# One attention layer on one core: q and k of a head pair in one PSUM bank, scores over 64 partitions, another start of the program

## The chip, the cores and the metric

The kernel runs on 1 core of a Trainium2 chip. The metric is device time in microseconds (us). The kernel before has 152.06 us as the median of 3 runs (151.92 to 152.91). Its profiled execution took 152.84 us, of which the span of the trace, from the first to the last instruction, is 151.1 us.

## The reference

One layer on a sequence of 256 rows, width 1024, 16 heads of 64:

```
hn   = rms_norm(x, norm_g)                 # x: (256, 1024) float32
q, k, v, z = split(hn @ w_in, 4)           # w_in: (1024, 4096)
s    = q k^T / 8 - slope_h * (t - s)       # causal, per head
o    = softmax(s) v
y    = x + (o * silu(z)) @ w_out           # w_out: (1024, 1024)
out  = rms_norm(y, final_g)
```

The sequence is one block of 256, so the choice of blocks in the reference never comes into play: every query sees its own block alone.

## The kernel before

Products are taken in float32 accuracy: each float32 operand is split into a high part, rounded to the type fp32r (ACT copies it), and a low part, the rest (DVE subtracts). A product is then three matmuls: high times high, high times low, low times high.

The work goes in four stages. **v**: x is transposed on PE (line 311), scaled by the norm weights `gT` on ACT (line 330) and split; eight rows of the v weights, 512 KB each, are loaded, split (lines 255 and 258) and multiplied, twelve products of 512 columns a row (lines 266 to 268). **z**: eight units of 128 columns of the gate weights, each 24 products of 256 columns (lines 271 to 273). **q, k and attention**: eight pairs of heads. A pair has a unit of q and a unit of k, 24 products each; then scores, softmax on DVE and ACT, transposes of the probabilities (line 447), the product with v (line 454). **o**: eight rows of `w_out`, their products cut into pieces of 512 and 256 columns, then the residual, the last norm and the stores.

How scores are made before: ACT rounds q, scaled by -1/8, into the tile `qq` on its own 64 partitions (line 399), DVE puts the low part of q on the other 64 partitions of the same tile (line 404). ACT rounds k into `kk` (line 408), a DMA on SP's queue copies `kk` to the other 64 partitions (line 412), DVE makes the low part `kl` (line 415), whose other half holds zeros. One matmul over 128 partitions then gives high and low part of q times the high part of k (line 424) and a second one high q times low k (line 425). Each head has two blocks (128 by 128, and 128 by 256), so a pair has 8 matmuls. q and k of a pair lie in two of three banks.

The order on every engine is written by a planner (`Plan`, lines 30 to 103): each piece of work has an engine, an estimated cost, a due time and what it reads and writes; the planner plays this through and the program is recorded in that order. Each engine then runs its own list strictly in order. SP's list holds most of the DMA issues, so an issue that waits holds those behind it.

Before the first product PE runs nine matmuls on a tile of zeros (`warm`, line 301), then transposes the norm weights (line 305) and the first quarter of x (line 311). The loads at the start are, on SP, the first quarter of x for rows 0 to 127 and the first weights; on ACT, the norm weights `gr` and then the first quarter of x for rows 128 to 255.

Of the kernel before, what the change touches and what calls it, by code (L numbers as in the profile page):

```python
# [22 lines left out]
EPS = 1e-6  # L23
MASKED = 3.0e38
HALF = (slice(0, DH), slice(DH, P))
# [81 lines left out]
def hybrid_trunk(ctx: ExitStack, tc: tile.TileContext, x, norm_g, w_in, w_out, final_g, out):  # L107
# [17 lines left out]
    def sb(name, shape, dtype=F32):  # L125
        return one.tile(shape, dtype, name=name)
# [18 lines left out]
    wl = [sb(f"wl{i}", [P, D], F32R) for i in range(NSPL)]  # L145
    NQ = 2
    qq = [sb(f"qq{i}", [P, 2, S], F32R) for i in range(NQ)]
    sb("pad3", [P, 16])
    kk = [sb(f"kk{i}", [P, 2, S], F32R) for i in range(NQ)]
    kl = [sb(f"kl{i}", [P, 2, S], F32R) for i in range(NQ)]  # L150
    NN = 3
# [7 lines left out]

    nc.sync.dma_start(xs[0][:, :256], x2[0:P, :256])  # L160
    nc.scalar.dma_start(gr, norm_g[0].rearrange("(t p) -> t p", p=P))
    nc.scalar.dma_start(xs[1][:, :256], x2[P:, :256])
    for i in range(2):
# [20 lines left out]
    def make_bias(h):  # L184
        nc.scalar.activation(bias[:, h, :], dist, AF.Copy, scale=2.0 ** (-8.0 * (h + 1) / H))

# [96 lines left out]

    def cols_unit(key, u, b, due):
        s = spl[key, u]
        h_, l_ = (w[s].rearrange("p (t e) -> p t e", t=ND) for w in (wh, wl))

        def step(g):
            for d in (2 * g, 2 * g + 1):
                mm3_cols(bank[b][:, :S], h_[:, d, :], l_[:, d, :], nh[:, d, :], nlo[:, d, :], d == 0, d == ND - 1)  # L290
        for g in range(4):
            add(T, 0.683, due + 0.683 * g, lambda g=g: step(g), split_of(s) + [("n", g)], [("b", b)], lat=0.25)
# [6 lines left out]
    slot["v", 0] = next_raw()  # L299
    for i in range(9):  # L300
        add(T, 0.21, -2000 + i, lambda: nc.tensor.matmul(bank[7][:, :256], warm[:, :P], warm, start=True, stop=True),
            [], [("b", 7)])

# [19 lines left out]

    add(T, 0.1, FIRST + 1, g_transpose, ["gr"], [("b", 6)], lat=0.25)
    add(V, 0.17, 0, lambda: nc.vector.tensor_copy(gT, bank[6][:, :ND]), [("b", 6)], ["gT"])
    for c in range(4):
        add(T, 0.45, FIRST if c == 0 else V0 + 2 * ROW * c - 2.3, lambda c=c: x_transpose(c), [("x", c, 0), ("x", c, 1)], [("b", 4 + c % 2)], lat=0.25)
        for d in (2 * c, 2 * c + 1):
# [49 lines left out]
    for i in range(ND):  # L378
        start = Z0 + UNIT * i
        if i % 2 == 0:  # L380
            load_cols("z", i, 3 * D + i * P, start - 12)
        split("z", i, cols_of("z", i), start, grid=ND)
        b = 4 + i % 2
        cols_unit("z", i, b, start)
        add(A, 0.42, start + UNIT + 1, lambda i=i, b=b: nc.scalar.activation(zs[:, i, :], bank[b][:, :S], AF.Silu),  # L385
            [("b", b), "silu"], [("zs", i)])
        if i == 0:
            add(G, 1.0, 5.0, make_dist, [("gh", 1)], ["dist"])
            for k in range(NQ):
                add(G, 0.5, 6.0 + k, lambda k=k: nc.gpsimd.memset(kl[k].bitcast(F32), 0.0), [("gh", 1)], [("kl", k), ("kl", k, 0), ("kl", k, 1)])  # L390
        for h in (2 * i, 2 * i + 1):
            add(A, 0.4, Z0 + 1.3 * h, lambda h=h: make_bias(h), ["dist"], [("bias", h)])
# [8 lines left out]
    def lo_q(p, b):  # L401
        t = qq[p % NQ]
        for a in range(2):
            nc.vector.scalar_tensor_tensor(t[HALF[1 - a], a, :], bank[b][HALF[a], :S], -(DH ** -0.5),
                                           t[HALF[a], a, :].bitcast(F32), op0=OP.mult, op1=OP.subtract)

    def hi_k(p, b, a):
        nc.scalar.copy(kk[p % NQ][HALF[a], a, :], bank[b][HALF[a], :S])  # L408
# [5 lines left out]
    def lo_k(p, b, a):  # L414
        nc.vector.tensor_sub(kl[p % NQ][HALF[a], a, :], bank[b][HALF[a], :S],  # L415
                             kk[p % NQ][HALF[a], a, :].bitcast(F32))

    def scores(p):

        for a in range(2):  # L420
            for o, q, k in ((slice(0, 128), slice(0, 128), slice(0, 128)),
                            (slice(128, 384), slice(128, 256), slice(0, 256))):
                l = qq[p % NQ][:, a, q]
                nc.tensor.matmul(bank[4 + a][:, o], l, kk[p % NQ][:, a, k], start=True, stop=False)  # L424
                nc.tensor.matmul(bank[4 + a][:, o], l, kl[p % NQ][:, a, k], start=False, stop=True)  # L425

    def softmax_max(p, a):
        for i, (o, b) in enumerate(BLK):
            nc.vector.tensor_tensor_reduce(nl[p % NN][:, a, o], bank[4 + a][:, o], bias[:, 2 * p + a, b], scale=1.0,  # L429
                                           scalar=3.0e38, op0=OP.add, op1=OP.min,  # L430
                                           accum_out=st[p % NN][:, 0, a, i:i + 1])
# [25 lines left out]
    for p in range(NP):  # L457
        base = A0 + PAIR * p
        if p % 2 == 0:
            load_cols("q", p, p * P, base - 12)  # L460
            load_cols("k", p, D + p * P, base - 9)
        bq, bk = (2 * p) % 3, (2 * p + 1) % 3
        split("q", p, cols_of("q", p), base, grid=ND)
        split("k", p, cols_of("k", p), base + UNIT, grid=ND)
        cols_unit("q", p, bq, base)
        cols_unit("k", p, bk, base + UNIT)
        E = base + 2 * UNIT + 0.3
        L = E - (0, 0, 0, 0, 0, 0, 3, 9)[p]
        n, m = p % NQ, p % NN
        add(A, 0.81, base + UNIT + 0.9, lambda p=p, b=bq: hi_q(p, b), [("b", bq)], [("qh", n)])  # L470
        add(V, 0.84, base + UNIT + 1.9, lambda p=p, b=bq: lo_q(p, b), [("b", bq), ("qh", n)], [("ql", n)])
        for a in range(2):
            add(A, 0.38, L + 0.4 + 0.4 * a, lambda p=p, b=bk, a=a: hi_k(p, b, a), [("b", bk)], [("kh", n, a)])
            add(Q, 0.2, L + 0.8 + 0.4 * a, lambda p=p, a=a: dup_k(p, a), [("kh", n, a)], [("kd", n, a)])
            add(V, 0.42, L + 1.0 + 0.4 * a, lambda p=p, b=bk, a=a: lo_k(p, b, a), [("b", bk), ("kh", n, a)],
                [("kl", n, a)])
        add(T, 0.97, FIRST + E, lambda p=p: scores(p),
            [("qh", n), ("ql", n)] + [(w, n, a) for w in ("kh", "kd", "kl") for a in range(2)] + [("kl", n)],
            [("b", 4), ("b", 5)], lat=0.25, slack=0.3)
        for a in range(2):  # L480
# [131 lines left out]
```

## Time and profile before

| | us |
|---|---|
| median of 3 runs | 152.06 |
| the profiled execution | 152.84 |
| its span | 151.1 |
| PE busy | 139.9 (93%) |
| DVE busy | 100.8 (67%) |
| ACT busy | 98.0 (65%) |
| POOL busy | 12.5 (8%) |

PE is TensorE's matmuls, PEld its weight loads. A matmul is pipelined: its own duration holds the way through the array, so what a matmul costs in a stream is the distance from its start to the start of the next one. In a timeline a row gives start, duration, engine, line, operation, tiles and shape, and in brackets how long the engine stood idle before it and what ended that.

### The profile page before, as it was taken

How to read it: one execution, taken by the hardware profiler on the slowest of the kernel's cores; microseconds unless marked ns; L12 is line 12 of the kernel's file. 1: busy time of each engine (PE TensorE's matmuls, PEld its weight loads, DVE VectorE, ACT ScalarE, POOL GpSimd, SP SyncE). 2: the span in 40 equal slices, each digit the busy share in tenths (PEclk: the TensorE clock that was granted, in tenths of full speed). 3: DMA queues.
4: the chain of work that ended last, by engine and by line, in shares of the span. 5: the costliest groups of instructions: out<-in, count | busy, mean ns of one | idle time of the engine just before them, and what ended most of it. 6: DMA issues, size and time to landing. Idle time of an engine off the chain costs nothing.

```text
span 151.1 us, 2711 instructions
## 1 busy us (share of the span) xinstructions
PE 139.9 (93%) x996; PEld 126.2 (84%) x996; DVE 100.8 (67%) x214; ACT 98.0 (65%) x217; POOL 12.5 (8%) x21
## 2 busy tenths in 40 slices
PE   7299999999999999999979999999999999999930
PEld 4178888889999999999959988998999788788820
DVE  0194899898534415686898786996867991653580
ACT  3294979888733617685974986779688863911240
POOL 6000010000000000000003001103010020150110
PEclk9999999999999999999999999999999999999995
DMA  4999999979886446717912481171000100000033
GB/s 115 336 401 404 369 369 348 348 248 284 258 255 157 149 105 209 245 35 196 386 47 93 184 274 43 35 278 34 9 20 17 39 0 0 0 0 4 0 139 139
DMA packets 18109, 24.82 MB, mean 164 GB/s; under 512 B 936, under 2 KB 15536, under 8 KB 18096
## 3 DMA queue, kind: packets, MB, share of 16 engines
q1 hardware_dynamic: 17792, 24.25, 49.3%
q10 hardware_dynamic: 304, 0.40, 0.8%
q8 instruction: 8, 0.13, 0.4%
q14 instruction: 5, 0.04, 0.1%
HBM read 22.55 MB, written 1.05 MB: 156 GB/s over the span
## 4 chain that ended last, share of the span: by engine, by line
PE 82%; DMA 7%; issue 3%; ACT 2%; DVE 1%; POOLq 0%; ACTq 0%; POOL 0%; DVEq 0%
PE bank L271 14%; PE bank L273 14%; PE bank L272 13%; PE bank L266 9%; PE bank L267 9%; PE bank L268 9%; DMA kk<-kk 5%; PE bank L454 4%; PE bank L447 3%; DMA xs<-in_x_dram 3%; PE bank L424 3%; PE bank L425 2%; PE bank L311 1%; ACT xs L542 1%; POOLq L607 0%
## 5 line engine op out<-in xcount | busy, mean ns | idle before, releaser
L258 DVE TENSOR_TENSOR wl<-raw,wh 128x1024 fp32r<-128x1024 f32 (+1 forms) x41 | 48.5, 1196 | 21.4 <-ACT wh L255 21.2
L271 PE MATMUL bank<-nh,wh 128*128 128x256 f32 x192 | 54.7, 285 | 0.0
L273 PE MATMUL bank<-nh,wl 128*128 128x256 f32 x192 | 53.5, 279 | 0.0
L272 PE MATMUL bank<-nlo,wh 128*128 128x256 f32 x192 | 53.5, 279 | 0.0
L255 ACT CAST wh<-raw 128x1024 fp32r<-128x1024 f32 (+1 forms) x41 | 41.5, 1026 | 0.9 <-PE bank L267 0.8
L271 PEld LDWEIGHTS bank<-nh,wh 128*128 128x128 f32 x192 | 36.0, 188 | 0.8 <-issue 0.7
L272 PEld LDWEIGHTS bank<-nlo,wh 128*128 128x128 f32 x192 | 36.0, 188 | 0.1
L273 PEld LDWEIGHTS bank<-nh,wl 128*128 128x128 f32 x192 | 36.1, 188 | 0.0
L266 PE MATMUL bank<-wh,gh 128*128 128x512 f32 (+1 forms) x72 | 28.2, 391 | 1.1 <-ACT wh L255 1.1
L267 PE MATMUL bank<-wh,gl 128*128 128x512 f32 (+1 forms) x72 | 27.2, 377 | 0.0
L268 PE MATMUL bank<-wl,gh 128*128 128x512 f32 (+1 forms) x72 | 27.1, 376 | 0.0
L266 PEld LDWEIGHTS bank<-wh,gh 128*128 128x128 f32 x72 | 14.1, 196 | 3.8 <-ACT wh L255 1.5
L499 POOL TENSOR_TENSOR gl<-gt,gh 128x256 fp32r<-128x256 f32 x8 | 8.3, 1032 | 106.2 <-ACT gh L497 106.2
L435 ACT ACTIVATE nl<-nl,st 128x128 f32<-128x128 f32 (+1 forms) x32 | 14.2, 447 | 3.2 <-DVE st L429 3.2
L268 PEld LDWEIGHTS bank<-wl,gh 128*128 128x128 f32 x72 | 13.9, 193 | 2.8 <-DVE wl L258 0.3
L267 PEld LDWEIGHTS bank<-wh,gl 128*128 128x128 f32 x72 | 14.0, 194 | 2.0
L385 ACT ACTIVATE zs<-bank 128x256 f32<-128x256 f32 x8 | 3.1, 385 | 11.5 <-PE bank L273 11.5
L429 DVE CUSTOM_DVE_ANT_0 nl<-bank,bias 128x128 f32<-128x128 f32 (+1 forms) x32 | 9.6, 352 | 0.7 <-PE bank L425 0.5
L491 ACT COPY pT<-bank 128x384 f32<-128x384 f32 x16 | 7.0, 483 | 4.0 <-PE bank L447 3.8
L408 ACT CAST kk<-bank 64x256 fp32r<-64x256 f32 x16 | 5.9, 367 | 5.2 <-PE bank L273 4.6
L415 DVE TENSOR_TENSOR kl<-bank,kk 64x256 fp32r<-64x256 f32 x16 | 6.8, 422 | 3.2 <-ACT kk L408 2.4
L399 ACT ACTIVATE qq<-bank 64x256 fp32r<-64x256 f32 x16 | 6.0, 377 | 4.1 <-PE bank L273 3.8
(66 smaller groups left out, 139.5 us busy)
## 6 DMA issues: line engine op xcount, KB each, us to landing
raw<-in_w_in_dram SPq DMA_DIRECT2D x12, 1024.0 KB, 7.4
raw<-in_w_out_dram SPq DMA_DIRECT2D x8, 512.0 KB, 4.5
raw<-in_w_in_dram SPq DMA_DIRECT2D x7, 512.0 KB, 5.7
kk<-kk SPq DMA_DIRECT2D x16, 64.0 KB, 2.0
xs<-in_x_dram SPq DMA_DIRECT2D x7, 128.0 KB, 5.1
raw<-in_w_in_dram SPq DMA_DIRECT2D x2, 256.0 KB, 4.2
fg<-in_final_g_dram SPq DMA_DIRECT2D x1, 512.0 KB, 10.1
out_dram<-raw SPq DMA_DIRECT2D x1, 512.0 KB, 2.6
```

What stands on the lines that cost most here:

```text
L255: add(A, 0.1 + 0.93 / parts, start - 3.0, lambda hi=hi, sr=sr: nc.scalar.copy(hi, sr), rw, [("wh", s, k) for k in ks])
L258: lambda lo=lo, hi=hi, sr=sr: nc.vector.tensor_sub(lo, sr, hi.bitcast(F32)),
L266: nc.tensor.matmul(acc, ah, bh, start=start, stop=False)
L267: nc.tensor.matmul(acc, al, bh, start=False, stop=False)
L268: nc.tensor.matmul(acc, ah, bl, start=False, stop=stop)
L271: nc.tensor.matmul(acc, ah, bh, start=start, stop=False)
L272: nc.tensor.matmul(acc, ah, bl, start=False, stop=False)
L273: nc.tensor.matmul(acc, al, bh, start=False, stop=stop)
L429: nc.vector.tensor_tensor_reduce(nl[p % NN][:, a, o], bank[4 + a][:, o], bias[:, 2 * p + a, b], scale=1.0, scalar=3.0e38, op0=OP.add, op1= ...
L435: nc.scalar.activation(nl[p % NN][:, a, o], nl[p % NN][:, a, o], AF.Exp, scale=-1.0, bias=st[p % NN][:, 0, a, i:i + 1], accum_out=st[p % N ...
L491: add(A, 0.45, L + 10 + 0.5 * a, lambda p=p, a=a, b=b: nc.scalar.copy(pT[p % 2][:, a, :], bank[b][:, :384]), [("b", b)], [("pT", p % 2, a)])
L499: lambda p=p: nc.gpsimd.tensor_sub(gl[:, p, :], gt[p % 2], gh[:, p, :].bitcast(F32)),
```

## The change

1. q and k of a pair are accumulated in the two halves of one bank. One ACT copy of 512 columns makes the high part of both (`qkh`), one DVE subtraction the low part (`qkl`). The scaled copy, the DMA that copies k, and the zeros on POOL are gone; the factor -1/8 moves into the softmax step on DVE, and the position bias is scaled to match. There are three buffers of these tiles in place of two.
2. Scores are three matmuls a block over the 64 partitions on which a head lies, in place of two over 128. The two heads of a pair alternate: 12 matmuls a pair in place of 8.
3. On ACT's queue the second part of x is issued ahead of the norm weights.
4. Ten matmuls on zeros stand at the start, two behind the transpose of the norm weights, and seven behind the transposes of the first quarter of x.

```diff
-MASKED = 3.0e38
+MASKED = 1.0e30
...
     nc.sync.dma_start(xs[0][:, :256], x2[0:P, :256])
+    nc.scalar.dma_start(xs[1][:, :256], x2[P:, :256])
     nc.scalar.dma_start(gr, norm_g[0].rearrange("(t p) -> t p", p=P))
-    nc.scalar.dma_start(xs[1][:, :256], x2[P:, :256])
...
-    def cols_unit(key, u, b, due):
+    def cols_unit(key, u, b, due, half=0):
...
-                mm3_cols(bank[b][:, :S], h_[:, d, :], l_[:, d, :], nh[:, d, :], nlo[:, d, :], d == 0, d == ND - 1)
+                mm3_cols(bank[b][:, half * S:half * S + S], h_[:, d, :], l_[:, d, :], nh[:, d, :], nlo[:, d, :], d == 0, d == ND - 1)
...
+    def keep_warm(n, due, reads=()):
+        for i in range(n):
+            add(T, 0.21, due + 0.01 * i, lambda: nc.tensor.matmul(bank[7][:, :256], warm[:, :P], warm,
+                                                                      start=True, stop=True), reads, [("b", 7)], lat=0.0)
+
+    keep_warm(10, -2000)
...
-    add(T, 0.1, FIRST + 1, g_transpose, ["gr"], [("b", 6)], lat=0.25)
+    add(T, 0.1, FIRST - 1, g_transpose, ["gr"], [("b", 6)], lat=0.25)
+    keep_warm(2, FIRST - 0.5, ["gr"])
     for c in range(4):
+        if c == 1:
+            keep_warm(7, FIRST + 2, [("b", 4)])
...
-    def hi_q(p, b):
-        for a in range(2):
-            nc.scalar.activation(qq[p % NQ][HALF[a], a, :], bank[b][HALF[a], :S], AF.Copy, scale=-(DH ** -0.5))
...
-    def dup_k(p, a):
-        t = kk[p % NQ].bitcast(F32)
-        nc.sync.dma_start(t[HALF[1 - a], a, :], t[HALF[a], a, :])
...
+    def hi_qk(p, b):
+        nc.scalar.copy(qkh[p % NQ].rearrange("p a s -> p (a s)"), bank[b])
+
+    def lo_qk(p, b):
+        nc.vector.tensor_sub(qkl[p % NQ].rearrange("p a s -> p (a s)"), bank[b],
+                             qkh[p % NQ].rearrange("p a s -> p (a s)").bitcast(F32))
 
     def scores(p):
-        for a in range(2):
-            for o, q, k in ((slice(0, 128), slice(0, 128), slice(0, 128)),
-                            (slice(128, 384), slice(128, 256), slice(0, 256))):
-                l = qq[p % NQ][:, a, q]
-                nc.tensor.matmul(bank[4 + a][:, o], l, kk[p % NQ][:, a, k], start=True, stop=False)
-                nc.tensor.matmul(bank[4 + a][:, o], l, kl[p % NQ][:, a, k], start=False, stop=True)
+        h_, l_ = qkh[p % NQ], qkl[p % NQ]
+        for o, q, k in ((slice(0, 128), slice(0, 128), slice(0, 128)),
+                        (slice(128, 384), slice(128, 256), slice(0, 256))):
+            for i, (l, r) in enumerate(((h_, h_), (h_, l_), (l_, h_))):
+                for a in range(2):
+                    nc.tensor.matmul(bank[4 + a][:, o], l[HALF[a], 0, q], r[HALF[a], 1, k],
+                                     start=i == 0, stop=i == 2)
...
-        bq, bk = (2 * p) % 3, (2 * p + 1) % 3
+        b = p % 3
...
-        cols_unit("q", p, bq, base)
-        cols_unit("k", p, bk, base + UNIT)
+        cols_unit("q", p, b, base)
+        cols_unit("k", p, b, base + UNIT, 1)
```

PE at the start, before: the transposes stand together behind the warm-up, then the first product.

```order
L301 MATMUL bank_128<-warm 128x256
L305 MATMUL bank_127<-ident,gr 128x8
L311 MATMUL bank_125<-ident,xs_63 128x128
L311 MATMUL bank_125<-ident,xs_64 128x128
L311 MATMUL bank_125<-ident,xs_63 128x128
L311 MATMUL bank_125<-ident,xs_64 128x128
L266 MATMUL bank_121<-wh_92,gh 128x512
```

The same place in the changed kernel (`xs_63` and `xs_64` are rows 0 to 127 and 128 to 255 of x):

```order
L300 MATMUL bank_127<-warm 128x256
L306 MATMUL bank_126<-ident,gr 128x8
L300 LDWEIGHTS warm
L300 MATMUL bank_127<-warm 128x256
L300 LDWEIGHTS warm
L300 MATMUL bank_127<-warm 128x256
L312 MATMUL bank_124<-ident,xs_63 128x128
L312 MATMUL bank_124<-ident,xs_64 128x128
L312 MATMUL bank_124<-ident,xs_63 128x128
L312 MATMUL bank_124<-ident,xs_64 128x128
L300 LDWEIGHTS warm
L300 MATMUL bank_127<-warm 128x256
```

Two warm-ups now stand between the transpose of `gr` and those of x, and seven (the first is the last row here) between these and the first product.

SP's queue where the copies of k begin, before (`raw` tiles take weights):

```order
L206 DMA raw_90<-in_w_in_dram 128x8x256
L412 DMA kk_105<-kk_105 64x256 x2
L206 DMA raw_86<-in_w_in_dram 128x8x256
L206 DMA raw_87<-in_w_out_dram 128x1024 x2
L412 DMA kk_106<-kk_106 64x256 x2
L412 DMA kk_105<-kk_105 64x256 x2
L206 DMA raw_88<-in_w_out_dram 128x1024 x2
```

And in the changed kernel:

```order
L204 DMA raw_90<-in_w_in_dram 128x8x256
L204 DMA raw_87<-in_w_out_dram 128x1024 x2
L204 DMA raw_86<-in_w_in_dram 128x8x256
L204 DMA raw_89<-in_w_out_dram 128x1024 x2
L204 DMA raw_88<-in_w_out_dram 128x1024 x2
L204 DMA raw_90<-in_w_out_dram 128x1024 x2
```

The copies are gone, and two loads of `w_out` have each moved ahead of another load.

PE near the end, before: the last products of the second piece (`bank_122`) of rows 0 to 127 of the output, and what follows. Behind these three rows of `bank_122` stand 4 groups of three products of 512 columns and 8 groups of 256.

```order
L266 MATMUL bank_122<-wh_101,gh 128x512
L267 MATMUL bank_122<-wh_101,gl 128x512
L268 MATMUL bank_122<-wl_101,gh 128x512
L266 MATMUL bank_123<-wh_98,gh 128x512
L267 MATMUL bank_123<-wh_98,gl 128x512
L268 MATMUL bank_123<-wl_98,gh 128x512
```

In the changed kernel the same piece lies in `bank_121`:

```order
L264 MATMUL bank_121<-wh_96,gh 128x512
L265 MATMUL bank_121<-wh_96,gl 128x512
L266 MATMUL bank_121<-wl_101,gh 128x512
L264 MATMUL bank_122<-wh_94,gh 128x512
L265 MATMUL bank_122<-wh_94,gl 128x512
L266 MATMUL bank_122<-wl_99,gh 128x512
```

Behind it stand 3 groups of 512 columns and 8 of 256, so this piece ends one group of 512 columns closer to the end. DVE's list at the end is the same in both.

## Rows read from the trace of the kernel before

**Rows 1.** The page: engines, busy us, share of the span, instructions.

```profile
PE 139.9 (93%) x996; PEld 126.2 (84%) x996; DVE 100.8 (67%) x214; ACT 98.0 (65%) x217; POOL 12.5 (8%) x21
```

**Rows 2.** Waits of PE: who waited for whom, us in total, times, longest.

```profile
PE bank L311 <- DMA xs<-in_x_dram: 1.7, 1, 1.7
PE bank L266 <- ACT wh L255: 1.1, 1, 1.1
...
PE bank L424 <- DMA kk<-kk: 0.9, 1, 0.9
```

**Rows 3.** The timeline of the first 13 us.

```profile
0.74 0.60 ACTq L161 DMA_DIRECT2D gr<-in_norm_g_dram  x1
0.74 0.39 SPq L160 DMA_DIRECT2D xs<-in_x_dram  x1
1.06 2.10 PE L301 MATMUL bank<-warm 128*128 128x256 bf16 x9 [1.06 <-DVE mhalf L171]
...
3.29 0.47 PE L311 MATMUL bank<-ident,xs 128*128 128x128 f32 x1
...
5.50 0.90 PE L311 MATMUL bank<-ident,xs 128*128 128x128 f32 x3 [1.73 <-DMA xs<-in_x_dram]
...
7.46 0.80 PE L266 MATMUL bank<-wh,gh 128*128 128x512 f32 x1 [1.07 <-ACT wh L255]
...
9.48 2.35 DVE L258 TENSOR_TENSOR wl<-raw,wh 128x1024 fp32r<-128x1024 f32 x2
...
12.63 0.39 PE L268 MATMUL bank<-wl,gh 128*128 128x512 f32 x1
```

**Rows 4.** The chain that ended last: start, us, what.

```profile
1.36 4.09 DMA xs<-in_x_dram
...
10.85 0.43 PE bank L267
...
11.88 0.23 PE bank L267
...
69.97 7.23 DMA kk<-kk
```

**Rows 5.** The timeline of PE around scores (67.8) and line 454 (78.4).

```profile
67.80 0.22 PE L424 MATMUL bank<-kk,qq 128*128 128x128 f32 x1
...
68.70 0.28 PE L271 MATMUL bank<-nh,wh 128*128 128x256 f32 x1
...
78.15 0.28 PE L425 MATMUL bank<-kl,qq 128*128 128x256 f32 x1
78.36 0.87 PE L454 MATMUL bank<-pT,v 128*64 128x256 f32 x8
79.16 0.39 PE L271 MATMUL bank<-nh,wh 128*128 128x256 f32 x1
79.39 0.28 PE L272 MATMUL bank<-nlo,wh 128*128 128x256 f32 x1
```

**Rows 6.** Groups by line, shapes apart: busy us, mean ns | idle before.

```profile
L268 PE MATMUL bank<-wl,gh 128*128 128x512 f32 x56 | 22.5, 402 | 0.0
L454 PE MATMUL bank<-pT,v 128*64 128x256 f32 x32 | 5.2, 405 | 0.0
...
L371 ACT ACTIVATE v<-bank,rstd 128x512 f32<-128x512 f32 x2 | 1.4, 687 | 0.6 <-PE bank L268 0.6
```

**Rows 7.** The end: timeline from 138 us on.

```profile
138.90 0.39 PE L266 MATMUL bank<-wh,gh 128*128 128x512 f32 x1
...
141.41 1.42 DVE L556 SCALAR_TENSOR_TENSOR raw<-raw,rf,fg 128x512 f32<-128x512 f32 x2 [0.66 <-POOL rf L553]
...
142.93 1.02 DVE L539 TENSOR_TENSOR raw<-bank,xs 128x512 f32<-128x512 f32 x2
...
144.40 0.28 PE L268 MATMUL bank<-wl,gh 128*128 128x256 f32 x1
...
144.72 0.42 DVE L539 TENSOR_TENSOR raw<-bank,xs 128x256 f32<-128x256 f32 x1 [0.17 <-PE bank L268]
```

More of the change, by code (lines that the diff above doesn't have):

```diff
@@ L145, in hybrid_trunk @@
     wl = [sb(f"wl{i}", [P, D], F32R) for i in range(NSPL)]
[L146 to L150, printed above, removed]
+    NQ = 3
+    qkh = [sb(f"qkh{i}", [P, 2, S], F32R) for i in range(NQ)]
+    qkl = [sb(f"qkl{i}", [P, 2, S], F32R) for i in range(NQ)]
     NN = 3
@@ L184, in make_bias @@
     def make_bias(h):
-        nc.scalar.activation(bias[:, h, :], dist, AF.Copy, scale=2.0 ** (-8.0 * (h + 1) / H))
+        nc.scalar.activation(bias[:, h, :], dist, AF.Copy, scale=-(DH ** 0.5) * 2.0 ** (-8.0 * (h + 1) / H))
     ROW, UNIT = 2.74, 2.73
@@ L299, in hybrid_trunk @@
     slot["v", 0] = next_raw()
-    for i in range(9):
-        add(T, 0.21, -2000 + i, lambda: nc.tensor.matmul(bank[7][:, :256], warm[:, :P], warm, start=True, stop=True),
-            [], [("b", 7)])
+    def keep_warm(n, due, reads=()):
[3 more added lines that the diff above has]
+    keep_warm(10, -2000)
     def g_transpose():
@@ L388, in hybrid_trunk @@
             add(G, 1.0, 5.0, make_dist, [("gh", 1)], ["dist"])
-            for k in range(NQ):
-                add(G, 0.5, 6.0 + k, lambda k=k: nc.gpsimd.memset(kl[k].bitcast(F32), 0.0), [("gh", 1)], [("kl", k), ("kl", k, 0), ("kl", k, 1)])
         for h in (2 * i, 2 * i + 1):
@@ L394, in hybrid_trunk @@
     dma(512, A0 - 12, fg, bass.AP(tensor=final_g.tensor, offset=final_g.offset, ap=[[0, P], [1, D]]), ["fg"])
-    def hi_q(p, b):
-        for a in range(2):
-            nc.scalar.activation(qq[p % NQ][HALF[a], a, :], bank[b][HALF[a], :S], AF.Copy, scale=-(DH ** -0.5))
-    def lo_q(p, b):
-        t = qq[p % NQ]
-        for a in range(2):
-            nc.vector.scalar_tensor_tensor(t[HALF[1 - a], a, :], bank[b][HALF[a], :S], -(DH ** -0.5),
-                                           t[HALF[a], a, :].bitcast(F32), op0=OP.mult, op1=OP.subtract)
@@ L407, in hi_k @@
-    def hi_k(p, b, a):
-        nc.scalar.copy(kk[p % NQ][HALF[a], a, :], bank[b][HALF[a], :S])
-    def dup_k(p, a):
-        t = kk[p % NQ].bitcast(F32)
-        nc.sync.dma_start(t[HALF[1 - a], a, :], t[HALF[a], a, :])
-    def lo_k(p, b, a):
-        nc.vector.tensor_sub(kl[p % NQ][HALF[a], a, :], bank[b][HALF[a], :S],
-                             kk[p % NQ][HALF[a], a, :].bitcast(F32))
-    def scores(p):
-        for a in range(2):
-            for o, q, k in ((slice(0, 128), slice(0, 128), slice(0, 128)),
-                            (slice(128, 384), slice(128, 256), slice(0, 256))):
-                l = qq[p % NQ][:, a, q]
-                nc.tensor.matmul(bank[4 + a][:, o], l, kk[p % NQ][:, a, k], start=True, stop=False)
-                nc.tensor.matmul(bank[4 + a][:, o], l, kl[p % NQ][:, a, k], start=False, stop=True)
+    def hi_qk(p, b):
+        nc.scalar.copy(qkh[p % NQ].rearrange("p a s -> p (a s)"), bank[b])
@@ L427, in softmax_max @@
     def softmax_max(p, a):
         for i, (o, b) in enumerate(BLK):
-            nc.vector.tensor_tensor_reduce(nl[p % NN][:, a, o], bank[4 + a][:, o], bias[:, 2 * p + a, b], scale=1.0,
+            nc.vector.tensor_tensor_reduce(nl[p % NN][:, a, o], bank[4 + a][:, o], bias[:, 2 * p + a, b], scale=-DH ** -0.5,
                                            scalar=3.0e38, op0=OP.add, op1=OP.min,
@@ L469, in hybrid_trunk @@
         n, m = p % NQ, p % NN
[L470 to L479, printed above, removed]
+        add(A, 0.63, L + 0.4, lambda p=p, b=b: hi_qk(p, b), [("b", b)], [("qkh", n)])
+        add(V, 0.70, L + 1.0, lambda p=p, b=b: lo_qk(p, b), [("b", b), ("qkh", n)], [("qkl", n)])
+        add(T, 0.95, FIRST + E, lambda p=p: scores(p), [("qkh", n), ("qkl", n)], [("b", 4), ("b", 5)],
+            lat=0.25, slack=0.3)
         for a in range(2):
```

## The prediction

> **What bounds the kernel now.** I read the busy times first: PE is busy for 93% of the span, DVE and ACT for about two thirds [rows 1]. A busy PE may still be waiting in small pieces, so the second view is the list of PE's own waits. Beside the wait for the first warm-up it has three entries: 1.7 us for the first part of x, 1.1 us for the first split weights, 0.9 us for the copy of k [rows 2]. From 7.46 us on PE therefore runs nearly without a gap, and time can only be won or lost in three ways: PE starts its products earlier, PE's stream gets shorter or longer, or the stretch behind its last product changes. Work taken from ACT, DVE, POOL or the DMA queues counts only where one of these waits goes.
>
> The third view is the timeline of the first 13 us [rows 3]. x for rows 128 to 255 lands 4.09 us after its issue at 1.36 us, at 5.45 us [rows 4], and PE's transposes wait for it. Then the products run, but not at their pace: the chain of waits gives 0.43 us for a product of 512 columns at 10.85 us and 0.23 us at 11.88 us [rows 4]. These are 512 columns at 1.2 and at 2.4 GHz. So about the first 3.8 us of products (7.46 to 11.3) ran at the lower of TensorE's two clocks, after a start in which PE had stood idle for 1.73 and 1.07 us between small pieces [rows 3].
>
> **The base.** The profiled execution took 152.84 us, 0.78 above the median of 152.06, and two of the three runs lie at the median or below. The terms below are differences; I set them against the median. Against the profiled execution itself the same sum gives 151.3 us.
>
> **The start.** Three edits act together. x for rows 128 to 255 is issued at 0.74 in place of 1.36 us. x for rows 0 to 127, issued on SP at 0.74, had landed by 3.29, when PE transposed it [rows 3]; the other half should now land at about that time too. But the norm weights go behind it, and their transpose and two warm-ups stand ahead of x on PE. Issued at about 1.1 us, they land at the earliest after the time they took before (issued 0.74, used before 3.29, so at most 2.55 us: 3.6 us), at the latest after the 4.09 us that x needed in this very place: 5.2 us. I take the middle, 4.3. Then PE does the small transpose (0.2), two warm-ups (nine took 2.10 us [rows 3], so 0.23 each), four transposes of x (0.9): done at 5.9, where it was 6.4. From there to the first product it took 1.06 us for scaling and splitting (6.4 to 7.46), which puts the first product at 7.0. The seven warm-ups in this gap fit in it at 2.4 GHz (0.8 us), but at 1.2 GHz they take 1.6 us and hold the product until 7.5.
>
> What they buy is the clock. PE then works without a gap from 4.3 us on. If the clock rises as long after that as it rose before after 7.46 (3.8 us), it does so at 8.1. The first row of weights has twelve products: 1.4 of them slow from 7.5 to 8.1, 10.6 at 0.23, ends at 10.5. Before, the second row's third product began at 12.63 [rows 3], two steps after its first, so the first row ended at 12.17. **Gain 1.6 us.** The best end is set by what comes next: the low part of the second row of weights, first half of the DVE entry at 9.48 of 2.35 us [rows 3], is ready at 10.7 and used by the product at 12.63. That is 1.9 us of room, some tenths more if ACT and DVE begin earlier: gain 2.2 at most. The worst end: norm weights at 5.2, seven slow warm-ups, no earlier clock; then the first row ends at 12.5, a loss of 0.4.
>
> **The copy of k.** The wait of 0.9 us for it goes [rows 2]; that DMA took 7.23 us, from 69.97 on [rows 4]. What is late next? In the changed order of PE the first scores stand five groups of six products behind the last of their k (3.5 us at 0.117 a product), the second ones four groups (2.8 us). In that time ACT must copy 512 columns out of PSUM (0.69 for such an operation [rows 6]) and DVE subtract as many (a 512 and a 256 column addition together took 1.02 [rows 7]): 1.5 to 1.7 us and the hand-overs. It fits. **Gain 0.9 us**; nothing if another wait stands in the same place. The four small ACT and four small DVE operations of a pair that become one each, the zeros on POOL, and the SP issues that no longer stand ahead of loads are costed at nothing, because PE waits for none of them; if PE lost this cover they would count as a gain.
>
> **Scores.** This is the open term, since PE pays for it in full, eight times. Before, the 8 matmuls of a pair take from 67.80 to 68.70, 0.90 us [rows 5], that is 0.1125 each although half of them have only 128 columns: the pace is that of the weight loads, one for each matmul. Now there are 12. If the two heads, on different halves of the array, run side by side, six loads set the pace: 6 x 0.1125 = 0.68. The trace has one operation with half of the array's columns, line 454. It fills the time from 78.27 (0.12 behind the start of the last score) to 79.27 (0.12 ahead of the row at 79.39), 1.00 us [rows 5]. Its eight passes are half of 256 columns, half of 128, and a pass of 256 lasts 405 ns, as long as a 512 column product, 402 [rows 6]. One after another these would need 4 x 0.23 + 4 x 0.117 = 1.39 us, more than the whole 1.00, so halves of the array do run side by side in this kernel. Side by side, in their order, I count about 0.8; the other 0.2 is lost where the shape changes: the load of line 454 is not ahead of the work, and the product behind it lasts 0.39 in place of 0.28 [rows 5]. With 0.2 to 0.4 for that, a pair's scores take 0.88 to 1.08; I take 0.96. **Loss 8 x 0.06 = 0.5 us.** The ends: the pace is set by columns alone (3 x 0.06 + 3 x 0.117 = 0.53, with 0.2 it is 0.73), a gain of 1.3; or twelve loads in series (1.35 with 0.2), a loss of 5.2.
>
> The Trainium skill speaks against this change here: by TensorEngine Tiling, Key Properties, a change of tiling mode (not merely of tile) drains TensorE, and scores now change it twice a pair. The trace agrees, with the 0.2 us around line 454. For the loads the skill has both: TensorE: Matmul & The Clock Gate, LDWEIGHTS, says that a load's time goes with its columns, whatever its rows (an estimate by its figure is 107 ns for 128 columns, near the 112 of the trace), by which twelve loads in series cost 1.3 us; the tiling page says that tiles load and multiply in parallel, by which it is half. No run here shows which.
>
> **The end.** The second piece of output rows 0 to 127 now ends one group of three 512 column products (0.69 us) closer to PE's end. Before, its last product was followed at 138.90 by the next group, and DVE had scaled these rows at 142.83 (141.41 and 1.42), 3.9 us later [rows 7]. PE's last step began at 144.40, 5.6 us after 138.90 with its own length; now it is 4.9. So DVE is free 1.0 us before PE ends, and needs 1.62 for what stands in its list ahead of the last addition (142.93 to 144.55; the addition then waited 0.17 for PE [rows 7]). The last addition begins 0.6 after PE's end in place of 0.2. **Loss 0.5 us**, with 0 and 0.7 (the whole group) as ends.
>
> **Sum:** -1.6 - 0.9 + 0.5 + 0.5 = -1.5; 152.06 - 1.5 = **150.6 us**, its own range 149.6 to 151.5.
>
> **Rivals.** *The loads run in series.* Then scores cost 8 x 0.65 = 5.2 us and the sum is -1.6 - 0.9 + 5.2 + 0.5 = +3.2: **155.3 us**, slower than before. It decides from 1.15 us for a pair on, where 8 x 0.25 eats the other terms. For it: weight loads already set the pace of the scores, one at a time at 0.1125. Against it: line 454's halves overlap, though in its matmuls, where loads can't be seen apart. *The start gives nothing:* norm weights land late, the clock rises where it did, and slow warm-ups hold the first product. Sum 0 - 0.9 + 0.5 + 0.5 = +0.1: **152.2 us**. For it: nine warm-ups up to 3.2 us did not prevent the slow products. Against: now less than a microsecond or so is left between warm-up and transposes. *All of it goes well:* gain 2.2 at the start, scores at the pace of their columns (-1.3), the end unchanged: -2.2 - 0.9 - 1.3 = -4.4, **147.7 us**. For it: loads into two halves need not cost twice. Against: it wants every bound at its best.
>
> **Chances.** Forecast 0.45, loads in series 0.20, start without gain 0.20, all well 0.15. About 1% (1.5 us) is what a measurement of this kernel can tell from no change: 150.5 and 153.6. The forecast's own range straddles the lower bound, a little over half below: 0.25 faster, 0.20 same. With the others: faster 0.25 + 0.15 = 0.40; same 0.20 + 0.20 + 0.02 (loads only partly in series) = 0.42; slower 0.18. The range goes from 148.0, near the best case, to 153.6, which leaves out the loads in series.
>
> **What would show it.** Right: the first product near 7.0 to 7.5 us with steps of 0.23 from about 8 us; a pair's scores from 0.88 to 1.08 us; no DMA `kk` in PE's waits; the last addition about half a microsecond behind PE's last product. Wrong: scores at 1.3 us or more; steps of 0.43 until 10 us or later; a new wait of PE for DVE's `qkl`; or PE waiting for split weights of the second row for longer than the 1.9 us of room allow.

## The result, and the profile after

The changed kernel takes **151.31 us** (median of 14 runs, 150.87 to 152.01); the kernel before, run beside it, takes 153.18 us (median of 14, 151.92 to 153.78). The ratio is 0.989 (95% interval 0.9864 to 0.9916), so the change saves 1.9 us or 1.1%. The forecast was 150.6 us, a gain of 1.5 from a base of 152.06. Between the two profiled executions, from which all the pieces below are taken, the gain is 152.84 - 151.30 = 1.54 us (spans 151.1 and 149.5).

The page's line on the engines, after, beside [rows 1]:

```profile
PE 141.4 (95%) x1038; PEld 125.6 (84%) x1038; DVE 94.5 (63%) x190; ACT 91.2 (61%) x193; POOL 9.9 (7%) x19
```

DVE lost 6.3 us of work and ACT 6.8, but past the first split weights PE waited for neither [rows 2], so this is not the gain. PE became busier by 1.5 us in a span that is 1.6 shorter: waits went. The list of PE's waits, after:

```profile
PE bank L300 <- DVE mhalf L169: 1.1, 1, 1.1
PE bank L306 <- DMA gr<-in_norm_g_dram: 0.3, 1, 0.3
PE bank L266 <- DVE wl L256: 0.2, 1, 0.2
```

Against [rows 2], the waits for x (1.7), for the first split weights (1.1) and for the copy of k (0.9) are gone. There is no wait for `qkl` or `qkh` in their place.

**The start.** The timeline of the first 11 us, after (start, us, engine, line, operation, tiles), to be held against [rows 3]:

```profile
0.74 0.41 ACTq L159 DMA_DIRECT2D xs<-in_x_dram  x1
...
1.17 0.59 ACTq L160 DMA_DIRECT2D gr<-in_norm_g_dram  x1
...
3.63 0.24 PE L306 MATMUL bank<-ident,gr 8*128 8x8 f32 x1 [0.26 <-DMA gr<-in_norm_g_dram]
...
4.21 1.06 PE L312 MATMUL bank<-ident,xs 128*128 128x128 f32 x4
...
6.41 0.75 PE L264 MATMUL bank<-wh,gh 128*128 128x512 f32 x1
...
7.55 0.40 PE L264 MATMUL bank<-wh,gh 128*128 128x512 f32 x1
7.79 0.39 PE L265 MATMUL bank<-wh,gl 128*128 128x512 f32 x1
...
10.44 0.50 PE L266 MATMUL bank<-wl,gh 128*128 128x512 f32 x1 [0.21 <-DVE wl L256]
```

The norm weights are there at 3.63, x is there when PE asks for it at 4.21, the first product starts at 6.41 in place of 7.46, and from 7.55 on a product of 512 columns takes a step of 0.23 us; before, that came at 11.47. The second row's third product starts at 10.44 in place of 12.63. The chain of waits says what holds it there:

```profile
2.11 5.95 DMA raw<-in_w_in_dram
8.08 1.06 ACT wh L253
9.16 1.24 DVE wl L256
10.44 0.50 PE bank L266
```

This is the second row of weights: loaded, rounded, split. The start is now bound by that load, which is the limit of 2.2 us that the prediction named. What the start is worth can be read at the first product of stage **z**, before and then after:

```profile
32.95 0.28 PE L271 MATMUL bank<-nh,wh 128*128 128x256 f32 x1
```

```profile
30.92 0.28 PE L269 MATMUL bank<-nh,wh 128*128 128x256 f32 x1
```

**Start: -2.03 us.** This figure can be some 0.4 off: in the nine other profiled executions with the new start (experiments 1 and 3 to 7) z begins between 30.34 and 31.19, and with the old start and the changed scores (experiment 1) it begins at 33.23. From this point to the start of PE's last matmul it took 144.40 - 32.95 = 111.45 us before and takes 142.61 - 30.92 = 111.69 now: **the middle, with the copy of k and all the scores, costs +0.24.** This figure is firmer: the five profiled kernels with the changed middle (this one, the scores alone of experiment 1, both of experiment 2 and that of experiment 6) all take 111.69 for it.

**Scores.** PE's timeline around the scores of one pair, after, beside [rows 5]:

```profile
65.66 0.28 PE L271 MATMUL bank<-nh,wl 128*128 128x256 f32 x1
65.86 0.33 PE L413 MATMUL bank<-qkh 64*128 64x128 f32 x2
66.03 0.27 PE L413 MATMUL bank<-qkl,qkh 64*128 64x128 f32 x2
...
66.54 0.28 PE L413 MATMUL bank<-qkh,qkl 64*128 64x256 f32 x2
66.75 0.39 PE L269 MATMUL bank<-nh,wh 128*128 128x256 f32 x1
66.98 0.28 PE L270 MATMUL bank<-nlo,wh 128*128 128x256 f32 x1
```

"x2" is the two heads, starting side by side; there are six such steps. Counted as line 454 was in the prediction, from 0.12 behind the start of the last product (65.78) to 0.12 ahead of the second one behind (66.86), a pair takes 1.08 to 1.09 us. The same count gives 0.90 to 0.93 before, where no wait stands in it. So +0.17 a pair, 1.36 for eight, less 0.2 at the one place where scores stand directly ahead of the product with v: **+1.16**.

**The copy of k.** The list of waits has 0.9 us of idle time for it, but PE lost more. Its timeline before shows the second pair, which waits, and the sixth, which does not:

```profile
76.06 0.28 PE L273 MATMUL bank<-nh,wl 128*128 128x256 f32 x1
77.25 0.33 PE L424 MATMUL bank<-kk,qq 128*128 128x128 f32 x1 [0.92 <-DMA kk<-kk]
...
107.84 0.28 PE L273 MATMUL bank<-nh,wl 128*128 128x256 f32 x1
107.96 0.22 PE L424 MATMUL bank<-kk,qq 128*128 128x128 f32 x1
...
108.97 0.87 PE L454 MATMUL bank<-pT,v 128*64 128x256 f32 x8
```

From the last product ahead of the scores to line 454 behind them it is 78.36 [rows 5] - 76.06 = 2.30 with the wait and 108.97 - 107.84 = 1.13 without: **-1.17**. With the scores' +1.16 that leaves -0.01 where the middle costs +0.24; the other 0.25 is not accounted for.

**The end,** after, beside [rows 7]:

```profile
141.63 1.02 DVE L522 TENSOR_TENSOR raw<-bank,xs 128x512 f32<-128x512 f32 x2
...
142.61 0.28 PE L266 MATMUL bank<-wl,gh 128*128 128x256 f32 x1
...
143.16 0.42 DVE L522 TENSOR_TENSOR raw<-bank,xs 128x256 f32<-128x256 f32 x1
```

The last addition starts 0.55 behind the start of PE's last matmul; before it was 144.72 - 144.40 = 0.32, with DVE waiting. Now DVE comes late: **+0.23**. Together -2.03 + 0.24 + 0.23 = -1.56, against 1.54 measured between the two executions.

### The profile page after: what moved, and what is told of

Same layout as the page of the kernel before. It is cut to its first block, busy times and chain, and to the rows that moved or that the text cites. A ratio compares the mean times of both kernels' runs of the same rounds, so it can differ in the third digit from the quotient of the medians.

```text
span 149.5 us, 2688 instructions
## 1 busy us (share of the span) xinstructions
PE 141.4 (95%) x1038; PEld 125.6 (84%) x1038; DVE 94.5 (63%) x190; ACT 91.2 (61%) x193; POOL 9.9 (7%) x19
## 4 chain that ended last, share of the span: by engine, by line
PE 85%; DMA 4%; issue 3%; DVE 2%; ACT 1%; SPq 1%; POOLq 0%; POOL 0%; DVEq 0%
PE bank L269 17%; PE bank L271 15%; PE bank L270 15%; PE bank L264 8%; PE bank L266 8%; PE bank L265 8%; PE bank L413 5%; PE bank L443 4%; DMA raw<-in_w_in_dram 4%; PE bank L436 4%; PE bank L312 1%; DVE wl L256 1%; ACT wh L253 1%; SPq L163 1%; ACT xs L525 0%
## 5 line engine op out<-in xcount | busy, mean ns | idle before, releaser
L269 PE MATMUL bank<-nh,wh 128*128 128x256 f32 x192 | 55.3, 288 | 0.0
L264 PE MATMUL bank<-wh,gh 128*128 128x512 f32 (+1 forms) x72 | 27.6, 383 | 0.0
L266 PE MATMUL bank<-wl,gh 128*128 128x512 f32 (+1 forms) x72 | 26.6, 370 | 0.2 <-DVE wl L256 0.2
L265 PE MATMUL bank<-wh,gl 128*128 128x512 f32 (+1 forms) x72 | 26.4, 367 | 0.0
L482 POOL TENSOR_TENSOR gl<-gt,gh 128x256 fp32r<-128x256 f32 x8 | 6.3, 789 | 108.6 <-ACT gh L480 108.6
L432 DVE TENSOR_TENSOR nl<-nl,st 128x256 f32<-128x256 f32 (+1 forms) x16 | 9.3, 622 | 0.3
L400 ACT CAST qkh<-bank 128x512 fp32r<-128x512 f32 x8 | 4.7, 583 | 7.2 <-PE bank L271 7.2
L443 PE MATMUL bank<-pT,v 128*64 128x256 f32 (+1 forms) x64 | 7.0, 339 | 0.0
```

Of the source, the lines that this page charges most:

```text
L264: nc.tensor.matmul(acc, ah, bh, start=start, stop=False)
L265: nc.tensor.matmul(acc, al, bh, start=False, stop=False)
L266: nc.tensor.matmul(acc, ah, bl, start=False, stop=stop)
L269: nc.tensor.matmul(acc, ah, bh, start=start, stop=False)
L432: nc.vector.tensor_mul(t, t, r[:, :, i:i + 1].to_broadcast([P, 2, o.stop - o.start]))
L443: nc.tensor.matmul(bank[7][HALF[a], o], v[:, j, h * DH:(h + 1) * DH], pT[p % 2][:, a, q], start=j == 0, stop=j == 1)
```

## The experiments

**1. The start alone, and the scores alone.** The first kernel is the one before with the three edits of the start, the second is the changed one without them.

```diff
+    nc.scalar.dma_start(xs[1][:, :256], x2[P:, :256])
     nc.scalar.dma_start(gr, norm_g[0].rearrange("(t p) -> t p", p=P))
-    nc.scalar.dma_start(xs[1][:, :256], x2[P:, :256])
...
+    keep_warm(10, -2000)
...
+    keep_warm(2, FIRST - 0.5, ["gr"])
...
+            keep_warm(7, FIRST + 2, [("b", 4)])
```

> The kernel before with the start of the changed one alone: second part of x ahead of the norm weights, warm-ups of 10, 2 and 7; scores and copies of k as before. Theory (the gain lies in the start alone, the middle comes out even): the third product of the second row of weights begins near 10.4 us in place of 12.6, and the whole is 1.9 us faster than before; the wait of PE for the copy of k stays at about 1 us, scores stay at 0.91 us a pair, the last addition begins right behind PE's end. Rival (the earlier start is given back behind, since the loads arrive no earlier): PE gets a new wait of 1 us or more before 35 us, and the whole gains under 1 us.

> The kernel before with the scores of the changed one alone: shared bank, one copy and one subtraction, 64 partitions, no copies of k; the start as before. Theory: the wait of 1.07 us goes, scores cost 1.09 in place of 0.92 us a pair (8 x 0.17 = 1.4 us, 0.2 of it saved where scores stand next to the product with v), the end loses 0.45 us: 0.4 us slower than before, between 0 and 0.8. Rival (relief of ACT, DVE and SP counts in the attention stage): 0.5 us or more faster than before.

Start alone: 151.28 us, ratio 0.9862 (0.9824 to 0.9900). Scores alone: 153.46 us, ratio 1.0016 (0.9986 to 1.0045). Both came as expected: the start alone gives what the whole change gives; the rest nets to nothing that can be measured. Why the two are even shows in PE's waits of the start alone:

```profile
PE bank L430 <- DMA kk<-kk: 1.3, 1, 1.3
```

The wait for the copy of k is still there, longer than before (the copy took 7.59 us), and its other scores take 0.90 to 0.93 us. The other half of the change takes this wait away and pays for it with slower scores and a later end.

**2. What in the start does it.** One kernel leaves out the warm-ups behind the transpose of `gr` and behind x, the other puts the norm weights back ahead of x.

```diff
-    keep_warm(2, FIRST - 0.5, ["gr"])
...
-        if c == 1:
-            keep_warm(7, FIRST + 2, [("b", 4)])
```

```diff
-    nc.scalar.dma_start(xs[1][:, :256], x2[P:, :256])
     nc.scalar.dma_start(gr, norm_g[0].rearrange("(t p) -> t p", p=P))
+    nc.scalar.dma_start(xs[1][:, :256], x2[P:, :256])
```

> The changed kernel without the nine late warm-ups (two behind the transpose of the norm weights, seven ahead of the first product); ten stand at the start. Theory (the warm-ups buy the clock, and the clock is most of the start's gain): the first product begins near 6.2 us, but steps of 0.43 last until about 8 to 10 us, so the second row's third product begins 0.5 to 1.5 us later than the 10.44 of the changed kernel, and the whole is slower by as much. Rival (the second row's weights arrive when they do, and PE waits for them in any case): within 0.3 us of the changed kernel.

> The changed kernel with the norm weights issued ahead of the second part of x again; all warm-ups stay. Theory (x early gives a first product one microsecond earlier, but the second row's weights bound the start): the first product begins at 7.2 to 7.6 us, at steps of 0.23 soon after, the second row's third product at 10.5 to 11.2; 0.1 to 0.7 us slower than the changed kernel. Rival (the order of the two loads is what made the gain): 1 us or more slower.

Without the late warm-ups: 152.05 us (151.22 to 152.79), ratio 0.9929 (0.9891 to 0.9966), 0.74 slower than the whole change. Norm weights first: 152.25 us (151.26 to 152.78), ratio 0.9922 (0.9891 to 0.9954), 0.94 slower, between what the two theories gave for it. PE's timeline without the late warm-ups:

```profile
5.84 0.80 PE L264 MATMUL bank<-wh,gh 128*128 128x512 f32 x1 [1.07 <-ACT wh L253]
...
8.16 0.63 PE L266 MATMUL bank<-wl,gh 128*128 128x512 f32 x1
8.59 0.49 PE L264 MATMUL bank<-wh,gh 128*128 128x512 f32 x1
8.92 0.40 PE L265 MATMUL bank<-wh,gl 128*128 128x512 f32 x1
```

and with the norm weights first:

```profile
5.55 0.90 PE L312 MATMUL bank<-ident,xs 128*128 128x128 f32 x3 [1.23 <-DMA xs<-in_x_dram]
...
7.60 0.78 PE L264 MATMUL bank<-wh,gh 128*128 128x512 f32 x1
...
8.60 0.63 PE L266 MATMUL bank<-wl,gh 128*128 128x512 f32 x1
9.03 0.45 PE L264 MATMUL bank<-wh,gh 128*128 128x512 f32 x1
```

Without warm-ups the first product is earlier still (5.84), but the steps are 0.43 until 8.6. With the norm weights first the wait for x is back (1.23), while the slow steps of 0.43 end at 9.0 instead of 11.1, and the second row's third product starts at 11.62. Each edit is worth about half: 0.9 for the order of the loads and 0.7 for the late warm-ups, from the medians. The execution shown without warm-ups is the fastest of its nine runs (151.22), as fast as the whole change: its second row's third product starts at 10.53, only 0.09 later, not the 0.5 to 1.5 that were expected. The profile doesn't show what its slower runs did, so that the late warm-ups gain their 0.7 by ending the slow steps sooner is argued, not shown. Whether the tenth warm-up at the very start matters was not tested. The runs spread over 1.6 and 1.5 us in these two kernels, 1.9 in the one before, and 1.1 in the changed kernel; as the middle takes 111.69 in both profiles, as in that of the changed kernel, the spread is likely to come from the start, but only one execution of each was profiled.

**3. How two heads share the array.** First the two inner loops of the scores are exchanged, so that one head's three matmuls stand ahead of the other's.

```diff
-            for i, (l, r) in enumerate(((h_, h_), (h_, l_), (l_, h_))):
-                for a in range(2):
+            for a in range(2):
+                for i, (l, r) in enumerate(((h_, h_), (h_, l_), (l_, h_))):
```

> The changed kernel with the two loops of the scores exchanged: in each block the three matmuls of one head, then the three of the other. Theory (neighbours on different halves of the array run side by side, loads too, and that is why 12 matmuls cost little more than 8): only one pair of neighbours in six is then on different halves, a pair's scores take 10 to 12 loads of 0.1125 and 0.4 for the change of shape, 1.5 to 1.75 us in place of 1.09, and the whole is 3.5 to 5 us slower than the changed kernel. Rival (a load of 64 rows simply takes half the time): 1.09 us a pair, no change.

My theory fell: 151.40 us in one run, 1.10 us a pair. PE's timeline of this kernel:

```profile
65.88 0.33 PE L413 MATMUL bank<-qkh 64*128 64x128 f32 x2
66.04 0.28 PE L413 MATMUL bank<-qkl,qkh 64*128 64x128 f32 x2
66.15 0.28 PE L413 MATMUL bank<-qkh,qkl 64*128 64x128 f32 x2
```

The program has three matmuls of one head, then three of the other; they run two at a time all the same. Alternating them in the program isn't what makes them overlap. That left two readings: the heads truly run side by side, or a load of 64 rows takes half the time and they go in turn. So one head was left out (its scores are not computed):

```diff
-                for a in range(2):
+                for a in range(1):
                     nc.tensor.matmul(bank[4 + a][:, o], l[HALF[a], 0, q], r[HALF[a], 1, k],
```

> The changed kernel with the second head's six matmuls left out of every pair's scores (that head's scores are not computed). Theory A (the two heads run side by side, each with its own loads, and one head alone needs the same time): a pair stays at 1.09 us, and the kernel's time does not move (within 0.6 us of 151.3). Theory B (two loads of 64 rows take half the time of one of 128 and go one after another): six loads fewer, 0.34 less a pair, 0.75 us, and 2.7 us less in all.

151.53 us in one run. PE's timeline:

```profile
65.77 0.28 PE L271 MATMUL bank<-nh,wl 128*128 128x256 f32 x1
65.98 0.33 PE L413 MATMUL bank<-qkh 64*128 64x128 f32 x1
66.14 0.27 PE L413 MATMUL bank<-qkl,qkh 64*128 64x128 f32 x1
...
66.65 0.27 PE L413 MATMUL bank<-qkh,qkl 64*128 64x256 f32 x1
66.86 0.39 PE L269 MATMUL bank<-nh,wh 128*128 128x256 f32 x1
```

"x1" now, and the same steps: 0.88 from the start of the first score (65.98) to the product behind (66.86), where two heads take 0.89 (65.86 to 66.75). The second head costs nothing. PE's weight loads in the changed kernel say the same:

```profile
65.86 0.19 PEld L413 LDWEIGHTS bank<-qkh 64*128 64x128 f32 x2
65.97 0.19 PEld L413 LDWEIGHTS bank<-qkl,qkh 64*128 64x128 f32 x2
```

Two loads start together at each step, and one of 64 rows lasts 0.19 us, as long as one of 128 rows (188 ns). Theory A holds: loads in series are excluded.

**4. Where the other 0.4 us of a pair goes.** All scores of a pair are made twice:

```diff
-        for o, q, k in ((slice(0, 128), slice(0, 128), slice(0, 128)),
-                        (slice(128, 384), slice(128, 256), slice(0, 256))):
+        for o, q, k in 2 * ((slice(0, 128), slice(0, 128), slice(0, 128)),
+                            (slice(128, 384), slice(128, 256), slice(0, 256))):
```

> The changed kernel with the 12 matmuls of a pair's scores issued twice, the second time over the first. Theory (of the 1.09 us a pair 0.68 is six paired loads and 0.4 the change of shape into and out of the halves, paid once for each visit): the second dozen costs 0.68 us a pair, a pair 1.77, the whole 5.4 us more than the changed kernel. Rival (there is no cost of the change of shape, and the dozen itself takes 1.09): 8.7 us more.

157.14 us in one run, 5.8 more than the changed kernel; a pair takes 1.77 us. PE's timeline, the second dozen and what follows:

```profile
66.92 0.22 PE L413 MATMUL bank<-qkh 64*128 64x128 f32 x2
...
67.49 0.28 PE L413 MATMUL bank<-qkh,qkl 64*128 64x256 f32 x2
67.70 0.38 PE L269 MATMUL bank<-nh,wh 128*128 128x256 f32 x1
```

The second dozen adds 1.77 - 1.09 = 0.68 us: the pace of six loads that the prediction gave. Eight times this is 5.4 of the 5.8; most of the rest lies ahead of z, which begins 0.26 later in this execution. The remaining 0.41 of a pair is paid once a visit, for going from the whole array to its halves and back.

**5. Paying the change of shape less often.** The product with v uses halves as well. In the first kernel the scores of six pairs stand directly ahead of the preceding pair's product with v (and the end has the edit of experiment 6); in the second those of three pairs (`JOIN` is 3, 4 and 5), with the end's code as it was. The cut is from the second; in the first the condition is `p < 2`.

```diff
+        if p not in JOIN:
+            add(T, 0.95, FIRST + E, lambda p=p: scores(p), r, w, lat=0.25, slack=0.3)
+        else:
+            add(T, 1.85, FIRST + E, lambda p=p: (scores(p), pv(p - 1)), r + pv_reads(p - 1), w + [("b", 7)],
+                lat=0.25, slack=0.3)
```

> The changed kernel with two edits: from the third pair on the scores of a pair and the product with v of the pair before stand next to each other on PE, so that one way back to the full array is saved (six such places, where the changed kernel has one); and the end as in e8_tail. Theory (the change of shape costs about 0.2 us each way): 5 x 0.2 = 1.0 us faster than e8_tail, less up to 0.5 at the end, where this order leaves less work of PE behind the first output rows. Rival (the shape costs nothing there, the 0.17 us a pair is in the loads): no faster than e8_tail.

> The changed kernel with the scores of pairs 3, 4 and 5 directly ahead of the preceding pair's product with v, which uses half of the array too. Theory (0.2 us of each change of shape is saved where two such stretches touch): three places at 1.89 in place of 2.09 us, 0.6 us faster than the whole change, if no new wait comes. Rival (as where six pairs were moved: the softmax has too little room): waits of PE for nl of more than 0.6 us, no gain or a loss.

Six pairs: 155.39 us, ratio 1.0164 (1.0079 to 1.0248). Each joined place does take 1.89 us instead of 1.09 + 1.00 = 2.09, but PE now waits, near the end, for the softmax. The profiled execution is the fastest of the four (153.95; the slowest took 156.49); its longest wait is:

```profile
127.03 0.30 PE L436 MATMUL bank<-ident,nl 128*128 128x128 f32 x1 [2.02 <-DVE nl L432]
```

Three pairs: 150.84 us, ratio 0.9853 (0.9818 to 0.9888), 0.47 under the changed kernel. The planner's order then has five joined places of 1.88 to 1.89 in place of one. The stretch from z to PE's last matmul is 141.39 - 30.74 = 110.65 us, 1.04 less than in the changed kernel (four more joined places at 0.2 are 0.8 of it; the rest is not accounted for), but the last addition begins at 142.63, 1.24 behind PE's last matmul in place of 0.55: the new order of the last pieces gives 0.7 back. So the saving at the joined places is shown, and an order of the end that keeps it was not tried.

**6. The end.** POOL multiplies the first half of the output by the final norm weights and ACT by the row factor, so that DVE is free for the last additions.

```diff
-                add(V, 0.75, due + 3 + t, lambda t=t, r=r, hs=hs, ys=ys: nc.vector.scalar_tensor_tensor(
-                    ys[t], hs[t], r, fg[:, t * 512:t * 512 + 512], op0=OP.mult, op1=OP.mult),
+                add(G, 1.6, due - 2 + 1.5 * t, lambda t=t, hs=hs, ys=ys: nc.gpsimd.tensor_mul(
+                    ys[t], hs[t], fg[:, t * 512:t * 512 + 512]), [("hh", j, t), "fg"], [("hf", t)])
...
+            add(A, 0.7, due + t, lambda t=t: nc.scalar.activation(ys0[t], ys0[t], AF.Copy, scale=r0),
```

> The changed kernel with the scaling of the first output rows taken off DVE: POOL multiplies by the final norm weights, ACT scales, behind ACT's squares; DVE then has only the additions in front of the last one. Theory (the last addition stood 0.45 us behind PE's end because DVE was scaling these rows): it begins right behind PE's end, and the whole is 0.4 to 0.5 us faster than the changed kernel. Rival (the later store of the first rows, or POOL beside DVE, costs as much): no change.

151.22 us, ratio 0.9876 (0.9829 to 0.9923): 0.1 less than the changed kernel, not 0.4 to 0.5. DVE's timeline of the end, PE's last matmul starting at 142.25 here:

```profile
142.56 0.42 DVE L522 TENSOR_TENSOR raw<-bank,xs 128x256 f32<-128x256 f32 x1 [0.40 <-PE bank L266]
```

DVE waits for PE again, and the last addition follows at 0.31, so the 0.24 of the end is undone. But the span (149.3) now ends 4.0 us behind the last store's issue (145.30) where it was 3.6 (149.5 and 145.92). From PE's last matmul to the end of the span it takes 7.1 us in place of 6.9: the edit gains nothing there, and this execution is the shorter one only because z began at 30.56, 0.36 earlier, ahead of all that was changed. The rows show that the store of the first half is now issued at 143.96, only 1.3 us ahead of the last one; that it is this which delays the last store is argued, not shown.

**7. A better version.** The wait for the copy of k can also be covered: the kernel before with the new start, and the second pair's scores placed later on PE, behind the first pair's product with v and 18 products more; then the fourth pair's too.

```diff
-            [("b", 4), ("b", 5)], lat=0.25, slack=0.3)
+            [("b", 4), ("b", 5)], lat=0.25, slack=3.5 if p == 1 else 0.3)
```

```diff
-            [("b", 4), ("b", 5)], lat=0.25, slack=0.3)
+            [("b", 4), ("b", 5)], lat=0.25, slack={1: 3.5, 3: 1.5}.get(p, 0.3))
```

> The kernel before with the new start alone, and the second pair's scores 18 matmuls (2.1 us) later in PE's order, so that the 7.6 us copy of k is there when they begin. Theory (the wait for this copy is a matter of where the scores stand, not of the bank or of the halves): the wait of 1.3 us that the start alone showed goes, nothing takes its place, 1.9 + 1.3 = 3.2 us faster than before, ratio 0.979, and 1.3 faster than the whole change. Rival (the later scores make the softmax late, and the transposes of the probabilities wait in their turn): 1.9 us faster than before, as the start alone. A wait of PE for nl or pT would show it.

> The kernel before with the new start and the scores of the second pair later, as in the run that waited 0.7 us for the copy of k at the fourth pair, and now the fourth pair's scores behind the third pair's product with v too, 1.0 us later. Theory: this wait goes as well, 0.7 us less than that run, 150.0 us, and PE waits for no copy of k any more, at 0.91 to 0.93 us a pair. Rival (the wait moves on to the next pair or to the transposes): the same as that run, 150.7 us, ratio 0.984.

The first: 150.70 us, ratio 0.9840 (0.9806 to 0.9873). The wait left the second pair, but the fourth pair met one, as its row in PE's timeline says:

```profile
87.49 0.30 PE L430 MATMUL bank<-kk,qq 128*128 128x128 f32 x1 [0.74 <-DMA kk<-kk]
```

Neither theory was quite right: somewhat under half of the 1.3 us came, and the wait moved on. The second: **150.00 us** (149.88 to 150.44), ratio 0.9813 (0.9777 to 0.9848), the fastest kernel here, 1.3 us under the changed one. All of its PE waits:

```profile
PE bank L302 <- DVE mhalf L171: 1.1, 1, 1.1
PE bank L308 <- DMA gr<-in_norm_g_dram: 0.2, 1, 0.2
```

No copy of k is waited for, though all sixteen are still made, and a pair's scores take 0.90 to 0.93 in seven places of eight (in the other they stand directly behind a product with v). So the copies themselves cost PE nothing; the place of two pairs' scores was.

## Why the prediction was near, and where it was off

The changed kernel came out 1.9 us faster by the medians and 1.54 by the profiled executions, against 1.5 forecast. The absolute number is 0.7 off because the three runs of the base lay low: their median was 152.06, that of the runs beside the result 153.18. The sum against the profiled execution, 151.3, is what was measured. Within the sum every term was off, by -0.4, -0.3, +0.7 and -0.3, and the middle has 0.25 more that no term holds. These cancel to less than 0.1: that the total fits is luck.

- **The start, -1.6 forecast, -2.03 measured.** The mechanism was right as far as the trace shows it: x early, shorter gaps on PE, steps of 0.23 sooner (what the last of these is worth alone stays open, experiment 2). The mis-sized part is the landing of the norm weights: I took 4.3 us, the middle between 3.6 and 5.2, and PE used them at 3.63. All that follows came as much earlier: first product 6.41 for 7.0, fast steps from 7.55 for 8.1. The bound of 2.2, set by the second row's split weights, held: that product now waits for them (0.21).
- **The copy of k, -0.9 forecast, -1.17 measured.** The wait went and nothing took its place, as forecast. The term took the idle time of the list for the price of the wait, and PE's stream lost 0.25 more. Experiment 7 adds that this gain was to be had without the new layout.
- **Scores, +0.5 forecast, +1.16 measured.** The part that I called open, six loads side by side, was right to the hundredth (0.68, experiments 3 and 4). The step that failed is the price of the change of shape: I took 0.28, between 0.2 and 0.4 from the surroundings of one operation, and it is 0.41 a visit. My range for a pair ended at 1.08; it is 1.09. The rows of the kernel before held nearly that much, and I misread them: I counted 0.8 for the eight passes of line 454 and 0.2 for the change. The trace has these passes two by two, starting at 78.36, 78.62, 78.84 and 78.95; a step is 0.22 for 256 columns and 0.11 for 128, so the passes need 0.65 of the 1.00 and the change of shape took 0.35.
- **The end, +0.5 forecast, +0.23 measured.** Right in kind: DVE is late, by its own list, not by PE. It was free 1.1 us before PE's end for 1.0, and needed 1.53 for 1.62. The forecast's own numbers give 0.4 (1.62 - 1.0, less the 0.2 of before), not 0.5.
- **The rivals.** *Loads in series* fell: one head takes as long as two. The rule of the Trainium skill (TensorEngine Tiling, Key Properties) that different tiles load and multiply in parallel agrees with this trace (0.88 us for one head, 0.89 for two). The rule of the Trainium skill in the same place that a change of tiling mode drains TensorE fits the 0.41 us a visit; that the loss is a drain no run here shows. *The start gives nothing* fell with experiment 1. *All goes well* had its start nearly (2.0 of 2.2), but scores never ran at the pace of their columns: six steps take 0.68, not 0.53.

The overall reading was thus right in sign, and in size by errors that cancel. It would have been a poor guide to what the edits are worth each: nearly the whole gain is the start, and the larger part of the diff, the scores, gives nothing.

## What to carry to other kernels

When a transfer is waited for, look first at where its consumer stands in the order: moving two pairs' scores brought no new wait and beat a new layout that did away with the transfer. Work on halves of the array is cheap while it lasts and pays for entering and leaving; put such stretches next to one another, and count visits, not matmuls. At the start of a program, what PE waits for first should be issued first, and PE should not stand idle between its first pieces.

## What was not expected of the hardware

- Matmuls on the two halves of the array's rows start side by side although the program has three of one half ahead of three of the other (experiment 3): two instructions that stand three apart ran at the same time (x2 at 65.88, 66.04 and 66.15).
- A change from the whole array to halves and back costs 0.41 us of PE's time a visit, twelve matmuls in between take 0.68, and two such stretches side by side save 0.2 (1.89 for 2.09).
- The granted clock reads 1.00 in the kernel before from 7.5 to 9.5 us, where the steps are 0.43, as it does from 11.4 to 13, where they are 0.23; the DMA share is 1.04 and 1.03. That the start runs at the lower clock (0.43 us is 512 columns at 1.2 GHz) is thus inferred from the steps alone, here as in the prediction; the record of the granted clock doesn't show it.
- The copies of k (64 KB each) that PE waited for took 4.96 to 7.59 us, with weight loads ahead of them on the same queue (before, the last of these landed at 77.01, the copy at 77.20); the median of the sixteen is 2.0 to 2.1 us.
